# A residual stream kept as fp32 tiles and updated in place, sums over h made from six classical tiles on, and the last output group by token halves

## The chip, the cores and the metric

The kernel runs on one core of one Trainium2 chip. The metric is the device time of one execution in microseconds (us). Before the change three runs gave 1734.82, 1736.02 and 1736.64 us; the median is 1736.02 us. Times in the trace are counted from the first instruction of one profiled execution of the same kernel.

## The reference, cut to what matters

A trunk of two layers over 528 tokens (16 meta tokens and 512 of the input) with 1024 channels, all in float32. Each layer has a mixer and an MLP, and after each of the four sublayers the stream is scaled, added to and normalized:

```python
DN_ALPHA = (2 * DEPTH) ** 0.25

def sq_relu_mlp(h, w1, w2):
    return jnp.square(jax.nn.relu(h @ w1)) @ w2        # w1 1024 x 4096, w2 4096 x 1024

for i in range(DEPTH):
    if i % 2 == 0:
        mix = retention_gdn_mixer(h, ...)              # retention heads and gated DeltaNet heads
    else:
        mix = mamba2_mixer(h, ...)                     # SSD
    h = layer_norm(DN_ALPHA * h + mix, ln1_w[i], ln1_b[i])
    h = layer_norm(DN_ALPHA * h + sq_relu_mlp(h, mlp_w1[i], mlp_w2[i]), ln2_w[i], ln2_b[i])
return h[:, N_META:]
```

## The kernel before, in words

**Numbers.** A value is kept as two rounded fp32 parts, hi and lo (`split`, L152 and L153: ScalarE casts hi, VectorE subtracts it to get lo). A product of two such values is three matmuls, hi by hi, hi by lo and lo by hi (`mm3`, L172 to L174). The activations lie with channels on the 128 partitions and tokens along the row: eight tiles `hh`/`hl` of 528 tokens. Layer 0 works in token halves of 272 and 256 tokens; from `wo1` on in layer 1 it is 256 and 256 (the 16 meta tokens are dropped), and there a matmul can take all 512 columns at once.

**Weights.** SyncE loads a weight tile of 128 x 1024 from HBM into a raw buffer of pool "w" (`fetch`, L160); `halve` then makes a hi and a lo buffer out of it, in the same pool. So a weight tile of 1024 columns takes three of the 12 buffers while it is split, and two until its last matmul. The normalizing rows (`row`) lie in a pool of 3 buffers of their own, and the work tiles `m` in a pool of 24.

**Order.** The code is one program text in which background tasks (generators) advance at each `tick`. A scheduler then lays the instructions of each engine in one fixed order, under the limits of the pools: a tile that finds no free buffer comes later in that order. Each engine works its own list strictly in that order; a row that waits holds up every row behind it on that engine. SyncE's list of DMA issues is such a list too.

**Norm** (`norm_after`). For each token half: transposes of the residual tiles (L270), statistics (L272, L294), scaled rows (L321 and L322), transposes back (L330), then hi by ScalarE (L337), the fp32 value by VectorE (L339) and lo by GpSimd or VectorE (L340). The residual `alpha * h` is rebuilt from hi and lo in `residual` (L354 and L355 ahead of time, or L366 and L367 at the first partial sum; later sums are added by L362).

**MLP** (`mlp`). The hidden layer of 4096 is cut into 8 groups of 4 tiles. Groups 0 and 1 are computed classically: w1 tiles 0 to 3 (the first three of them by token halves, held, as `head=3`), then for each tile of group 1 the tile itself and two output tiles of w2 for group 0 (`second(0, ...)`). From group 2 on, two hidden tiles at a time are computed by a scheme of seven products in place of eight (`Unit`, its matmuls at L500); for it VectorE and GpSimd make four sums over h for each of four row pairs (`combos`, L386 to L401, 16 sums, each split into hi and lo, called `tt`) and four sums over the weights (L473 to L477). A unit's first product needs a weight part and h alone; its second needs the weight sum s2 and the sums over h. Between units stand `Four` stages: four output tiles of w2 for the group before. The last group's output (`second(NG - 1, ..., tail=3)`) takes five tiles whole and the last three by token halves, so that the norm of half 0 runs beside the products of half 1.

**Around it.** The mixer of layer 0 has 40 weight tiles of 1024 x 128 and ends with `wo0` (8 output tiles with two weight loads each, the last two by token halves, `tail=2`); GDN's triangular solve goes through HBM (`da`, `dt`, `du`, L776 to L813, with rows in pool "row"). The SSD mixer of layer 1 reads rows of decay factors back from HBM (`rd`, L1171), and ends with `wo1`.

Of the kernel before, what the change touches and what calls it, by code (L numbers as in the profile page):

```python
# [18 lines left out]
P = 128  # L19
# [38 lines left out]
def trunk(ctx: ExitStack, tc: tile.TileContext, a, out):  # L58
# [11 lines left out]
    NBUF = {"s": 40, "m": 24, "n": 40, "row": 3}  # L70
# [84 lines left out]
    def wtile(dt=F32R):  # L155
        return sb.tile([P, 1024], dt, tag="w", bufs=12, name=nm("w"))
# [152 lines left out]
    def norm_after(r, ns, wcol, bcol):  # L309
# [5 lines left out]
        def task(hf):  # L315
            n, norm = ns[hf], []

            def apply(off, bn, pt, mean, rstd):
                row = tl("row", 1024)
                t2 = [row[:, j * 512:(j + 1) * 512] for j in range(2)]  # L320
                S.activation(t2[1][:bn], pt[1][:bn, :], AF.Identity, bias=shift(mean, rstd, bn), scale=rstd)  # L321
                V.tensor_scalar(t2[0][:bn], pt[0][:bn, :], mean, rstd, op0=SUB, op1=MUL)  # L322
# [4 lines left out]
            for m in range(KT):  # L327
# [10 lines left out]
                t = tl("m", n)  # L338
# [7 lines left out]
    def residual(hx, offs, ns, early=()):  # L346

        r, pre = [{}, {}], [{}, {}]
        for m in early:
            for hf in range(2):  # L350
                n, off = ns[hf], offs[hf]
                hi, lo = hx[hf][m]
                t = tl("m", n)
                V.tensor_scalar(t, hi[:, off:off + n].bitcast(F32), DN_ALPHA, None, op0=MUL)  # L354
                V.scalar_tensor_tensor(t, lo[:, off:off + n].bitcast(F32), DN_ALPHA, t, op0=MUL, op1=ADD)  # L355
                pre[hf][m] = t

        def evac(m, hf, o, last=True):
            n, off = ns[hf], offs[hf]
            if m in pre[hf]:  # L360
                t = pre[hf][m]
                V.tensor_tensor(t, t, o, op=ADD)  # L362
            else:
                hi, lo = hx[hf][m]
                t = pre[hf][m] = tl("m", n)
                V.scalar_tensor_tensor(t, hi[:, off:off + n].bitcast(F32), DN_ALPHA, o, op0=MUL, op1=ADD)  # L366
                V.scalar_tensor_tensor(t, lo[:, off:off + n].bitcast(F32), DN_ALPHA, t, op0=MUL, op1=ADD)  # L367
# [4 lines left out]
    def combos(pairs, nh, get):


        q = slice(0, nh), slice(nh, 2 * nh)

        def part(k, c, lo):
            return pairs[k][lo][:, q[c]].bitcast(F32)

        def diff(out, a, b, engine):  # L380
            engine.tensor_tensor(out, a, b, op=SUB)

        for k in range(4):
            d1, d3, e = tl("m", nh), tl("m", nh), tl("m", nh)
            G.tensor_tensor(d1, part(k, 1, 0), part(k, 0, 0), op=SUB)
            V.tensor_tensor(e, part(k, 1, 1), part(k, 0, 1), op=SUB)  # L386
            V.tensor_tensor(d1, d1, e, op=ADD)
            get(0, k, d1)
            yield
            G.tensor_tensor(d3, part(k + 4, 1, 0), part(k, 1, 0), op=SUB)  # L390
            V.tensor_tensor(e, part(k + 4, 1, 1), part(k, 1, 1), op=SUB)
            V.tensor_tensor(d3, d3, e, op=ADD)
            get(2, k, d3)
            yield
            d2, d4 = tl("m", nh), tl("m", nh)
            G.tensor_tensor(d2, part(k + 4, 1, 0), d1, op=SUB)
            V.tensor_tensor(d2, d2, part(k + 4, 1, 1), op=ADD)
            get(1, k, d2)
            yield
            G.tensor_tensor(d4, part(k + 4, 0, 0), d2, op=SUB)  # L400
            V.tensor_tensor(d4, d4, part(k + 4, 0, 1), op=ADD)  # L401
            get(3, k, d4)
            yield

    def mlp(l, hx, ns, ready, r, evac0, pairs):
# [155 lines left out]
        u, ev = group()  # L561
        phase([([w1[l, f]], f) for f in range(GF)], hx, ev, ns, head=3, ready=ready)
        spawn(combos(pairs, nh, get))
        stages = []
        un, evn = group()
        groups = [(u, ev), (un, evn)] + [group() for _ in range(2, NG)]
# [213 lines left out]
    def gdn_base():  # L780
# [3 lines left out]
        bt, tb, ub = [tl("row", n * n, part=68) for _ in range(3)]  # L784
# [19 lines left out]
        tms = [tl("row", 1024) for _ in range(2)]  # L804
# [317 lines left out]
    r, ev = residual(h, (0, 0), ns0, early=range(5, KT))  # L1122
# [40 lines left out]
    def ssd_group(g, f, ys):  # L1163
# [5 lines left out]
        def loads(c):  # L1169
            rw = tl("row", 1024)  # L1170
# [177 lines left out]
    r, ev = residual(h, (16, 0), ns1, early=range(5, KT))  # L1348
# [18 lines left out]
    r, ev = residual(h, (0, 0), ns1)  # L1367
# [3 lines left out]
    def finish(hf):  # L1371
# [5 lines left out]
        def whole(off, bn, pt, mean, rstd):  # L1377
            row = tl("row", 1024)
# [34 lines left out]
    mlp(1, h, ns1, ready, r, ev, hp)  # L1413
# [101 lines left out]
```

## Time and profile before

| what | value |
|---|---|
| median of the runs shown | 1736.02 us |
| the profiled execution | 1738.46 us |
| its span, first to last instruction | 1736.7 us |
| around the span | 1.8 us |
| mean granted TensorE clock | 0.982 |
| DMA, over the span | 158.05 MB, 91 GB/s |

The profile's page gives first the busy time of each engine: PE is TensorE's matmuls, PEld its weight loads, DVE VectorE, ACT ScalarE, POOL GpSimd, SP SyncE. A row of a timeline has the start, the duration, the engine, the line of the kernel, the operation, the tiles written and read, and how many records were put together; in brackets stands the idle time ahead of it and what ended it. A row of the windows has, for a stretch of time, its length, the busy time of PE, PEld, DVE, ACT and POOL with counts, the granted clock as a share of full speed, the busy share of the DMA engines and GB/s.

### The profile page before, as it was taken

To read this page: it belongs to the slowest core of one execution; us is meant where nothing else is said; L and a number is where in the kernel's file an instruction comes from. 1 tells how busy PE (TensorE), PEld (TensorE's weight loads), DVE (VectorE), ACT (ScalarE), POOL (GpSimd) and SP (SyncE) were. 2 spreads that over 40 slices of the span, in tenths; PEclk is the share of its full clock that TensorE was granted. 3 is DMA by queue.
4 is the path that set the end of the run, shared out by engine and by line. 5 is a ranking of instruction groups with operands and counts; after the bars stand their busy time and mean duration, and the time that the engine had idled before them with its cause. 6 is when DMAs were issued, how large, how long until landed. Compare 5 with 4: busy or idle time off the path is not lost.

```text
span 1736.7 us, 30064 instructions
## 1 busy us (share of the span) xinstructions
PE 1674.2 (96%) x11896; PEld 1542.2 (89%) x11896; DVE 1199.8 (69%) x2383; ACT 700.9 (40%) x1354; POOL 351.1 (20%) x412
## 2 busy tenths in 40 slices
PE   9998999999999899999999998999999998999997
PEld 7897998899999889999998987888778987888886
DVE  5896666766437877767747876767564688777765
ACT  4432235554214344444424643545432434444431
POOL 1211210010003411111102145344410342111112
PEclk9998999999999999999999999999999999999999
DMA  7223212112222232222221443333223123222321
GB/s 243 82 91 86 88 47 84 46 54 84 87 74 68 73 104 98 98 98 98 79 71 62 137 121 92 102 112 98 91 67 110 55 91 110 98 98 98 101 73 69
DMA packets 93002, 158.05 MB, mean 91 GB/s; under 512 B 14077, under 2 KB 47229, under 8 KB 92605
## 3 DMA queue, kind: packets, MB, share of 16 engines
q1 hardware_dynamic: 92716, 155.87, 27.9%
q8 instruction: 93, 1.52, 0.4%
q14 instruction: 49, 0.39, 0.1%
q10 hardware_dynamic: 144, 0.26, 0.0%
HBM read 149.95 MB, written 6.15 MB: 90 GB/s over the span
## 4 chain that ended last, share of the span: by engine, by line
PE 79%; DVE 10%; DMA 4%; POOL 3%; ACT 2%; issue 2%; SPq 0%; POOLq 0%; DVEq 0%; ACTq 0%
PE pmm L172 18%; PE pmm L174 18%; PE pmm L173 18%; PE pmx L500 10%; PE pmm L500 4%; DVE w L153 2%; DVE s L603 2%; DMA row<-rd 1%; DMA w<-in_w 1%; PE pmx L1241 1%; PE pmx L270 1%; DMA du<-row 1%; POOL n L147 1%; PE pmx L1245 1%; ACT w L152 1%
## 5 line engine op out<-in xcount | busy, mean ns | idle before, releaser
L172 PE MATMUL pmm<-hh,w 128*128 128x256 f32 (+5 forms) x1528 | 472.9, 310 | 5.6 <-DVE m L366 2.8
L174 PE MATMUL pmm<-hh,w 128*128 128x256 f32 (+5 forms) x1528 | 459.4, 301 | 2.1 <-DVE w L153 2.1
L173 PE MATMUL pmm<-hl,w 128*128 128x256 f32 (+5 forms) x1528 | 458.4, 300 | 0.7 <-POOL hl L340 0.3
L153 DVE TENSOR_TENSOR w<-w,w 128x1024 fp32r<-128x1024 f32 (+2 forms) x269 | 323.7, 1205 | 142.0 <-PE pmm L173 67.6
L152 ACT CAST w<-w 128x1024 fp32r<-128x1024 f32 (+2 forms) x269 | 263.7, 981 | 373.7 <-PE pmm L174 137.1
L172 PE MATMUL pmm<-s,w 128*128 128x256 f32 (+2 forms) x1180 | 376.8, 319 | 4.3 <-DVE m L366 2.7
L174 PE MATMUL pmm<-s,w 128*128 128x256 f32 (+2 forms) x1180 | 375.5, 318 | 0.2 <-DVE w L153 0.2
L173 PE MATMUL pmm<-s,w 128*128 128x256 f32 (+2 forms) x1180 | 375.5, 318 | 0.0
L172 PEld LDWEIGHTS pmm<-hh,w 128*128 128x128 f32 (+2 forms) x1528 | 289.1, 189 | 20.9 <-issue 4.0
L173 PEld LDWEIGHTS pmm<-hl,w 128*128 128x128 f32 (+2 forms) x1528 | 289.0, 189 | 13.5 <-issue 2.4
L174 PEld LDWEIGHTS pmm<-hh,w 128*128 128x128 f32 (+2 forms) x1528 | 289.0, 189 | 11.4 <-DVE w L153 2.9
L172 PEld LDWEIGHTS pmm<-s,w 128*128 128x128 f32 x1180 | 222.3, 188 | 20.1 <-DVE m L366 3.2
L174 PEld LDWEIGHTS pmm<-s,w 128*128 128x128 f32 x1180 | 222.2, 188 | 15.8 <-DVE w L153 0.6
L173 PEld LDWEIGHTS pmm<-s,w 128*128 128x128 f32 x1180 | 222.2, 188 | 15.2 <-DVE s L1320 0.3
L435 POOL TENSOR_TENSOR m<-m 128x256 f32<-128x256 f32 (+2 forms) x128 | 89.0, 697 | 511.7 <-ACT m L433 499.4
L362 DVE TENSOR_TENSOR m<-m,pmm 128x256 f32<-128x256 f32 (+1 forms) x236 | 93.6, 416 | 71.7 <-PE pmm L174 71.5
L147 POOL TENSOR_TENSOR n<-n,neg 128x1 f32<-128x1 f32 (+2 forms) x58 | 39.8, 690 | 450.4 <-DVE n L146 426.4
L603 DVE SCALAR_TENSOR_TENSOR s<-s,pp,s 128x528 f32<-128x528 f32 x120 | 101.3, 844 | 33.4 <-ACT s L601 31.1
L442 DVE TENSOR_TENSOR s<-m,s 128x256 fp32r<-128x256 f32 (+2 forms) x128 | 69.5, 546 | 51.1 <-POOL m L435 49.9
L500 PE MATMUL pmx<-s,s 128*128 128x264 f32 (+1 forms) x576 | 75.4, 287 | 5.6 <-ACT s L152 5.3
L500 PEld LDWEIGHTS pmx<-s,s 128*128 128x128 f32 x576 | 72.5, 192 | 6.1 <-ACT s L152 5.5
L500 PE MATMUL pmx<-s,w 128*128 128x264 f32 (+1 forms) x576 | 77.6, 284 | 0.0
(312 smaller groups left out, 2368.1 us busy)
## 6 DMA issues: line engine op xcount, KB each, us to landing
w<-in_w SPq DMA_DIRECT2D x88, 512.0 KB, 3.3
w<-in_mw SPq DMA_DIRECT2D x176, 256.0 KB, 3.0
w<-in_mw SPq DMA_DIRECT2D x40, 512.0 KB, 3.2
w<-in_wo SPq DMA_DIRECT2D x29, 512.0 KB, 3.4
row<-rd SPq DMA_DIRECT2D x16, 512.0 KB, 5.7
s<-rd SPq DMA_DIRECT2D x32, 128.0 KB, 5.5
out<-row SPq DMA_DIRECT2D x7, 256.0 KB, 2.0
w<-in_wo SPq DMA_DIRECT2D x6, 256.0 KB, 2.5
```

Source lines behind the costliest of these rows:

```text
L147: G.tensor_tensor(dst, t, neg5[0:part, 0:n], op=POW)
L152: S.copy(dst_hi, src)
L153: V.tensor_tensor(dst_lo, src, dst_hi.bitcast(F32), op=SUB)
L172: T.matmul(o, w[0], x[0], start=first, stop=False)
L173: T.matmul(o, w[0], x[1], start=False, stop=False)
L174: T.matmul(o, w[1], x[0], start=False, stop=last)
L270: T.transpose(pt[m // 4][:bn, (m % 4) * P:(m % 4 + 1) * P], r[m][:, off:off + bn], ident)
L362: V.tensor_tensor(t, t, o, op=ADD)
L435: G.tensor_tensor(q, t, t, op=MUL)
L442: V.tensor_tensor(lo, q, hi.bitcast(F32), op=SUB)
L500: T.matmul(o, w[x][:, c], B[b][k][y], start=first and k == i == 0, stop=last and k == 3 and i == 2, skip_group_check=True)
L603: V.scalar_tensor_tensor(acc, cin[:, k:k + L], w[k], acc, op0=MUL, op1=ADD)
```

## The change

Eight fp32 tiles `R` of 128 x 528 hold the residual stream from start to end. They are loaded with the input, the first partial sum of a sublayer does `R = alpha * R + sum` in one VectorE instruction, later ones add, and the norm writes its fp32 result back into them. The sums over h are then made from R by four VectorE instructions for each row pair, none on GpSimd. For the room, pool "m" goes from 24 to 19 buffers, and pool "row" (3) is merged with pool "w" (12) into one of 13. In the MLP only six w1 tiles stay classical (group 0, and tiles 0 and 2 of group 1); tiles 1 and 3 of group 1 become a 13th unit, and the output of group 0 moves behind it into two `Four` stages. The last group's weights are prepared as `Four` stages are, and all eight of its output tiles go by token halves.

```diff
-    NBUF = {"s": 40, "m": 24, "n": 40, "row": 3}
+    NBUF = {"s": 40, "m": 19, "n": 40, "w": 13}
...
-        return sb.tile([P, 1024], dt, tag="w", bufs=12, name=nm("w"))
+        return sb.tile([P, 1024], dt, tag="w", bufs=NBUF["w"], name=nm("w"))
...
+    R = [sb.tile([P, L], F32, tag="r", bufs=KT, name=nm("r")) for _ in range(KT)]
...
-            raw = tl("m", n)
+            raw = R[k][:, o:o + n]
...
-                row = tl("row", 1024)
+                row = tl("w", 1024)
...
-                t = tl("m", n)
+                t = r[hf][m]
                 V.tensor_scalar(t, pf, w, b, op0=MUL, op1=ADD)
...
         def evac(m, hf, o, last=True):
-            n, off = ns[hf], offs[hf]
-            if m in pre[hf]:
-                t = pre[hf][m]
+            t = R[m][:, offs[hf]:offs[hf] + ns[hf]]
+            if (m, hf) in seen:
                 V.tensor_tensor(t, t, o, op=ADD)
             else:
-                hi, lo = hx[hf][m]
-                t = pre[hf][m] = tl("m", n)
-                V.scalar_tensor_tensor(t, hi[:, off:off + n].bitcast(F32), DN_ALPHA, o, op0=MUL, op1=ADD)
-                V.scalar_tensor_tensor(t, lo[:, off:off + n].bitcast(F32), DN_ALPHA, t, op0=MUL, op1=ADD)
+                V.scalar_tensor_tensor(t, t, DN_ALPHA, o, op0=MUL, op1=ADD)
+                seen.add((m, hf))
...
+    def combos(off, nh, get):
 
         for k in range(4):
...
+            q0, q1 = [[R[i][:, off + c * nh:off + (c + 1) * nh] for c in range(2)] for i in (k, k + 4)]
+            d = [tl("m", nh) for _ in range(4)]
+            V.tensor_tensor(d[0], q0[1], q0[0], op=SUB)
+            V.tensor_tensor(d[2], q1[1], q0[1], op=SUB)
+            V.tensor_tensor(d[1], q1[1], d[0], op=SUB)
+            V.tensor_tensor(d[3], q1[0], d[1], op=SUB)
...
+        stages = [unit(1, 1), four(0, 0), four(0, 1)]
         for c in range(2, NG):
...
-        for f in range(GF):
-            phase([([w1[l, GF + f]], f)], hx, evn, ns)
-            if f == 2:
-                spawn(stages[0].gen)
-            second(0, u, 2 * f, 2 * f + 2)
+            stages += [unit(c, 0), four(c - 1, 0), unit(c, 1), four(c - 1, 1)]
+        last = [four(NG - 1, 0), four(NG - 1, 1)]
+        gens = [st.gen for st in stages + last]
+        phase([([w1[l, f]], f) for f in range(GF)], hx, groups[0][1], ns, head=3, ready=ready)
+        spawn(combos(off, nh, get))
+        phase([([w1[l, GF]], 0)], hx, groups[1][1], ns)
+        spawn(gens[0])
+        phase([([w1[l, GF + 2]], 2)], hx, groups[1][1], ns)
         until(lambda: "s4" in stages[0].ops and all(x is not None for y in tt for x in y))
...
-        second(NG - 1, groups[-1][0], 0, KT, tail=3)
+        blks = last[0].blks + last[1].blks
+        phase([([[blks[m]]], m) for m in range(KT)], groups[-1][0], evac0, ns, tail=KT)
...
-        zero = tl("row", 731)
+        zero = tl("w", 731)
...
-        bt, tb, ub = [tl("row", n * n, part=68) for _ in range(3)]
+        bt, tb, ub = [tl("w", n * n, part=68) for _ in range(3)]
...
-            rw = tl("row", 1024)
+            rw = tl("w", 1024)
```

The same rename from "row" to "w" is made in the output's norm. Over the whole program TensorE streams 3,223,300 matmul columns in place of 3,229,540; VectorE has 2281 instructions in place of 2365, ScalarE 1293 in place of 1301, GpSimd 385 in place of 417.

**TensorE at the end of wo0, where the MLP of layer 0 begins.** In this list `pmm_6352` of before (`pmm_6306` of the change) is the last output tile of wo0, `pmx` with `cst` are transposes of the norm for token half 1, and `hh`/`hl` with `w` are the MLP's w1 products. Before, in the order of TensorE:

```order
L270 MATMUL pmx_6473<-cst,m_5391 128x128
L172 MATMUL pmm_6352<-s_5353,w_6194 128x256
L173 MATMUL pmm_6352<-s_5354,w_6194 128x256
L174 MATMUL pmm_6352<-s_5353,w_6195 128x256
L172 MATMUL pmm_6538<-hh_6381,w_6534 128x272
L173 MATMUL pmm_6538<-hl_6382,w_6534 128x272
L174 MATMUL pmm_6538<-hh_6381,w_6535 128x272
```

The change, the same place:

```order
L174 MATMUL pmm_6306<-s_5345,w_6149 128x256
L272 MATMUL pmx_6408<-cst,r_81 128x128
...
L332 MATMUL pmx_6517<-cst,w_6468 128x128
L332 MATMUL pmx_6523<-cst,w_6468 128x128
...
L332 MATMUL pmx_6559<-cst,w_6468 128x128
L332 MATMUL pmx_6559<-cst,w_6473 128x128
L172 MATMUL pmm_6484<-hh_6335,w_6480 128x272
```

Before, three w1 half tiles (72 matmuls, `pmm_6538`, `pmm_6638`, `pmm_6677`) stand between wo0's last matmul and the end of the norm's transposes of half 1; in the change none does, and `pmm_6484` follows the last transpose. Its weight's hi part, on ScalarE, and lo part, on VectorE, stand among the norm's rows of half 1 (ScalarE: behind the sixth of eight hi rows).

**VectorE in the classical phase of the MLP, layer 0, the change.** `L414` makes the lo part of a hidden tile's square and so waits for that tile's products; `s_6847` is made from `pmm_6817`, the first half of the fifth of six classical w1 tiles and the ninth of their twelve half tiles on TensorE. `L441` to `L445` are the unit's weight sums, `L368` to `L371` the sums over h.

```order
L153 TENSOR_TENSOR w_7055<-w_6956,w_7054 128x1024
L414 TENSOR_TENSOR s_6847<-m_6844,s_6846 128x272
L368 TENSOR_TENSOR m_6850<-r_75 128x264
L369 TENSOR_TENSOR m_6852<-r_79,r_75 128x264
L370 TENSOR_TENSOR m_6851<-r_79,m_6850 128x264
...
L371 TENSOR_TENSOR m_7029<-r_82,m_7027 128x264
L153 TENSOR_TENSOR s_7037<-m_7027,s_7037 128x264
L153 TENSOR_TENSOR w_7106<-w_7062,w_7105 128x1024
L153 TENSOR_TENSOR s_7041<-w_6957,s_7040 128x512
```

All 16 sums over h stand behind that `L414`; from the first of them to `s_7041`, the lo part of the weight sum s2, there are 36 rows: 16 sums, 14 of their splits, 3 rows `L414`, one row `L445`, the split of `w_7106` and that of s2 itself, which is the last. In layer 1 the list has the same form with 256 columns; there the second `L414` row of `s_16052`, which waits for the last of the six classical tiles, stands in the middle of it, and 17 rows follow it up to the lo part of s2 (7 sums, 7 of their splits, one `L445`, the split of a 1024-column weight and that of s2). Before, the sums of a layer are spread over the list between the rows of eight w1 and eight w2 tiles.

**SyncE in layer 0's mixer.** `da` is the scratch of GDN's solve in HBM, and `w` from `in_w` are weight tiles. The change:

```order
L749 DMA da<-s_938 128x4x128
L758 DMA w_981<-da 68x32x32
L160 DMA w_1053<-in_w 128x1024
L160 DMA w_1150<-in_w 128x1024
L160 DMA w_1249<-in_w 128x1024
```

Before, the load of the same weight tile, there `w_1061`, stands ahead of the writes:

```order
L160 DMA w_1061<-in_w 128x1024
L160 DMA w_1158<-in_w 128x1024
L776 DMA da<-s_734 128x4x128
...
L776 DMA da<-s_946 128x4x128
L160 DMA w_1495<-in_w 128x1024
L785 DMA row_989<-da 68x32x32
```

Six weight loads that stood ahead of the read of `da` stand behind it. They are `w_1061`, `w_1158`, `w_1257`, `w_1352`, `w_1420` and `w_1495` before, `w_1053` to `w_1487` in the change.

More of the change, by code (lines that the diff above doesn't have):

```diff
@@ L370, in residual, with mlp @@
         return r, evac
[L372 to L381, printed above, removed]
-        for k in range(4):
[L384 to L405, printed above, removed]
+    def combos(off, nh, get):
+        for k in range(4):
+            q0, q1 = [[R[i][:, off + c * nh:off + (c + 1) * nh] for c in range(2)] for i in (k, k + 4)]
[4 more added lines that the diff above has]
+            V.tensor_tensor(d[3], q1[0], d[1], op=SUB)
+            for j in range(4):
+                get(j, k, d[j])
+                if j % 2:
+                    yield
+    def mlp(l, hx, off, ns, ready, evac0, pairs):
         w1, w2 = a["mw1"], a["mw2"]
@@ L559, in run, with unit, four @@
                             adv()
[L561 to L566, printed above, removed]
-        for c in range(2, NG):
-            for i in range(2):
-                stages.append(Unit(c, i, lambda f, hf, o, e=groups[c][1]: e(f, hf, o, nh)))
-                stages.append(Four(c - 1, groups[c - 1][0], 4 * i))
-        for f in range(GF):
-            phase([([w1[l, GF + f]], f)], hx, evn, ns)
-            if f == 2:
-                spawn(stages[0].gen)
-            second(0, u, 2 * f, 2 * f + 2)
+        groups = [group() for _ in range(NG)]
+        def unit(c, i):
+            return Unit(c, i, lambda f, hf, o: groups[c][1](f, hf, o, nh))
+        def four(c, i):
+            return Four(c, groups[c][0], 4 * i)
+        stages = [unit(1, 1), four(0, 0), four(0, 1)]
+        for c in range(2, NG):
+            stages += [unit(c, 0), four(c - 1, 0), unit(c, 1), four(c - 1, 1)]
[6 more added lines that the diff above has]
+        phase([([w1[l, GF + 2]], 2)], hx, groups[1][1], ns)
         until(lambda: "s4" in stages[0].ops and all(x is not None for y in tt for x in y))
@@ L803, in gdn_base @@
         yield from pause(2)
-        tms = [tl("row", 1024) for _ in range(2)]
+        tms = [tl("w", 1024) for _ in range(2)]
         for hd in range(4):
@@ L1121, in trunk @@
     ns0 = (272, 256)
-    r, ev = residual(h, (0, 0), ns0, early=range(5, KT))
+    r, ev = residual((0, 272), ns0)
     hn, hp, ready = norm_after(r, ns0, PP_LN, PP_LN + 8)
@@ L1125, in trunk @@
     h = hn
-    r, ev = residual(h, (0, 0), ns0)
+    r, ev = residual((0, 272), ns0)
     hn, hx, ready1 = norm_after(r, ns0, PP_LN + 16, PP_LN + 24)
-    mlp(0, h, ns0, ready, r, ev, hp)
+    mlp(0, h, 0, ns0, ready, ev, hp)
     h = hn
@@ L1347, in trunk @@
     srcs = [[a["wo1"][m, :, 0:1024], a["wo1"][m, :, 1024:2048]] for m in range(KT)]
-    r, ev = residual(h, (16, 0), ns1, early=range(5, KT))
+    r, ev = residual((16, 272), ns1)
     hn, hp, ready = norm_after(r, ns1, PP_LN + 32, PP_LN + 40)
@@ L1366, in trunk @@
     h = hn
-    r, ev = residual(h, (0, 0), ns1)
+    r, ev = residual((16, 272), ns1)
     normed = [False, False]
@@ L1377, in whole @@
         def whole(off, bn, pt, mean, rstd):
-            row = tl("row", 1024)
+            row = tl("w", 1024)
             t0, t1 = row[:, 0:512], row[:, 512:1024]
@@ L1388, in last @@
         def last(blocks):
-            t = [[x[:, 0:512], x[:, 512:1024]] for x in (tl("row", 1024), tl("row", 1024))]
+            t = [[x[:, 0:512], x[:, 512:1024]] for x in (tl("w", 1024), tl("w", 1024))]
             (o0, p0, m0, n0, s0), (o1, p1, m1, n1, s1) = blocks
@@ L1412, in trunk @@
     spawn(finish(1))
-    mlp(1, h, ns1, ready, r, ev, hp)
+    mlp(1, h, 16, ns1, ready, ev, hp)
     drain()
```

30 lines of the change are left out of this document (10 added, 20 removed).

## The prediction

> **What bounds the kernel now.** The page comes first: its busy times and its chain of work.
>
> ```profile
> span 1736.7 us, 30064 instructions
> PE 1674.2 (96%) x11896; PEld 1542.2 (89%) x11896; DVE 1199.8 (69%) x2383; ACT 700.9 (40%) x1354; POOL 351.1 (20%) x412
> PE 79%; DVE 10%; DMA 4%; POOL 3%; ACT 2%; issue 2%; SPq 0%; POOLq 0%; DVEq 0%; ACTq 0%
> ```
>
> TensorE is busy for 1674.2 of 1736.7 us, so about 62 us of the span are gaps. A change gains only by fewer matmul columns or fewer gaps. Next, the view that lists TensorE's waits by what it waited for: the largest single ones.
>
> ```profile
> PE pmx L1006 <- ACT m L1027: 8.0, 1, 8.0
> PE pmm L172 <- DVE m L366: 5.6, 5, 1.5
> PE pmx L500 <- ACT s L152: 5.3, 1, 5.3
> ```
>
> The first lies in layer 0's mixer, the second in the classical part of layer 0's MLP, the third at the first unit of layer 1's MLP. The windows show what stands beside them.
>
> ```profile
> 150.00:160.00 10.00, 2.42 (x18) 2.09 (x16) 0.79 (x3) 1.10 (x2) 0.00 (x0) 0.74 0.74 214
> ...
> 590.00:600.00 10.00, 8.55 (x68) 8.13 (x67) 10.00 (x23) 3.84 (x9) 4.36 (x6) 1.00 0.01 2
> 600.00:610.00 10.00, 6.57 (x48) 5.75 (x46) 9.58 (x17) 3.20 (x7) 4.66 (x6) 1.00 0.22 79
> 610.00:620.00 10.00, 6.58 (x32) 6.37 (x33) 5.95 (x12) 2.56 (x5) 0.17 (x1) 0.66 0.08 26
> ...
> 1430.00:1440.00 10.00, 7.43 (x37) 5.80 (x35) 8.92 (x18) 3.66 (x8) 5.05 (x6) 1.00 0.58 190
> 1440.00:1450.00 10.00, 6.80 (x36) 6.50 (x37) 8.95 (x19) 4.63 (x8) 0.73 (x1) 0.66 0.07 25
> ```
>
> In the classical part of both MLPs VectorE is the limit (10.00 and 9.58 of 10 us at 590 to 610, with TensorE down to 6.57). The column of the granted clock shows a second price: after a gap of some microseconds the clock stands at 0.66 over 10 us, so 3.4 us are not granted, part of them inside the gap. I charge 2.6 us of half clock for a long gap (bounds 1.7 and 3.4).
>
> **Matmuls.** The chain gives a unit's products; two starts of a 512-column tile give the classical step.
>
> ```profile
> 693.69 1.46 PE pmm L500 x12
> 695.15 4.41 PE pmx L500 x36
> ...
> 1507.77 1.41 PE pmm L500 x12
> 1509.18 4.26 PE pmx L500 x36
> ...
> 1430.02 0.39 PE L172 MATMUL pmm<-s,w 128*128 128x512 f32 x1
> 1430.25 0.40 PE L173 MATMUL pmm<-s,w 128*128 128x512 f32 x1
> ```
>
> One matmul of a unit takes 4.41/36 = 0.122 us in layer 0 and 4.26/36 = 0.118 us in layer 1; 512 columns take about 0.225 us (0.23 between these starts, 0.22 and 0.23 alternating). The 13th unit is 84 matmuls. It replaces 96 of about 0.122 in layer 0 (11.7 to 10.2, gain 1.5) and 48 of 0.225 in layer 1 (10.8 to 9.9, gain 0.9). The last group of layer 1 by halves takes 24 x 0.118 = 2.83 in place of 12 x 0.225 = 2.70 us a tile; five more tiles do so: **+0.7**. These gains are inside the two sums below.
>
> **From the norm into the MLP, layer 0.** The order shows that no w1 product stands any more beside the norm of half 1: 72 matmuls, some 9 us, that covered it have moved behind its last transpose, because raw, hi and lo of the first weight find no free buffer among 13 while wo0's last two tiles hold eight and the norm's rows the others. What the norm takes is in the trace:
>
> ```profile
> 539.95 0.29 PE L172 MATMUL pmm<-hh,w 128*128 128x272 f32 x1
> ...
> 541.11 0.40 DVE L362 TENSOR_TENSOR m<-m,pmm 128x256 f32<-128x256 f32 x1
> 541.43 1.21 DVE L153 TENSOR_TENSOR w<-w,w 128x1024 fp32r<-128x1024 f32 x1
> ...
> 544.38 1.03 ACT L152 CAST w<-w 128x1024 fp32r<-128x1024 f32 x1
> 548.89 3.76 ACT L337 ACTIVATE hh<-pmx,pp 128x256 fp32r<-128x256 f32 x8 [0.33 <-PE pmx L330]
> ```
>
> Before, TensorE went from wo0 to w1 at 539.95. From the last evacuation at 541.11 to the first hi row is 7.8 us. The change takes the weight split of 1.21 us out of that stretch, and transposes no longer queue behind products (0.7, an estimate): first hi row at 547.0. Six hi rows (6 x 0.47 = 2.8), the weight's cast (1.03) and its split (1.21 less overlap) put the first full w1 step at **551.7**. That is a gap of almost 10 us with only transposes in it; I charge 2.0 us of clock. Twelve half tiles of 24 matmuls at 0.1225 (between 256 and 272 columns), 12 x 2.94 = 35.3 us, then end at 589.0, and the unit's first product (1.5) at 590.5.
>
> **The unit's second product, layer 0.** It needs the sums over h and s2. VectorE reaches them only behind the `L414` of the ninth half tile: 551.7 + 2.0 + 9 x 2.94 = 580.2, plus 1.4 us for relu, square and lo. Then come 36 rows. Their price:
>
> ```profile
> 582.39 0.42 DVE L386 TENSOR_TENSOR m<-hl 128x264 f32<-128x264 f32 x1
> 582.73 0.43 DVE L367 SCALAR_TENSOR_TENSOR m<-hl,m 128x272 f32<-128x272 f32 x1
> 583.09 0.42 DVE L387 TENSOR_TENSOR m<-m,m 128x264 f32<-128x264 f32 x1
> ...
> 585.13 0.68 DVE L153 TENSOR_TENSOR w<-w,w 128x512 fp32r<-128x512 f32 x1
> 585.73 0.87 DVE L153 TENSOR_TENSOR s<-m,s 128x264 fp32r<-128x264 f32 x1
> ...
> L153 DVE TENSOR_TENSOR s<-m,s 128x264 fp32r<-128x264 f32 x11 | 5.4, 502 | 0.5 <-ACT s L152 0.5
> ```
>
> A row of 264 columns takes 0.42 us and the next begins 0.35 after it; a 512-column split 0.60, a 1024-column one 1.13 by the same measure. 33 rows x 0.345 + 2 x 0.60 + 1.13 = 13.7 us. In the same phase the splits average 0.502 us beside GpSimd (one row above: 0.87), so I add 1.8: 15.5 us (bounds 13.7 and 36 x 0.502 = 18). s2 is ready at 597.1. TensorE waits from 590.5: **6.6 us**, 2.6 of clock, then 72 matmuls (8.8) and eight w2 tiles of 24 (23.3, four of them already done in the gap, 0.5 less). Group 2 begins at 631.3. Before:
>
> ```profile
> 627.57 0.28 PE L500 MATMUL pmm<-hh,w 128*128 128x264 f32 x1
> ...
> 1367.23 0.40 DVE L362 TENSOR_TENSOR m<-m,pmm 128x256 f32<-128x256 f32 x1
> 1373.42 3.76 ACT L337 ACTIVATE hh<-pmx,pp 128x256 fp32r<-128x256 f32 x8 [0.27 <-PE pmx L330]
> ...
> 1437.36 0.28 PE L500 MATMUL pmm<-hh,w 128*128 128x256 f32 x1
> 1442.93 0.79 PE L500 MATMUL pmx<-s,s 128*128 128x256 f32 x2 [5.30 <-ACT s L152]
> ```
>
> Layer 0: 631.3 - 627.6 = **+3.7 us** (range -2 to +9). This already counts that the old gaps of 590 to 614 are gone.
>
> Three or four of GpSimd's squares fall into that stretch. The Trainium skill, SBUF — State Buffer, section "SBUF: two separate sides", says that VectorE with two SBUF inputs and GpSimd lock a shared port for a whole instruction. The 0.87 us row above agrees with it. By it, GpSimd's 32 subtractions that leave would free VectorE, the 1.8 us would go in each layer, and the sum would be 3.6 us lower; it would still be positive.
>
> **The same in layer 1.** Hi rows began at 1373.42; with the split out, 1372.3, plus 2.8, 1.03 and 0.8: first step at 1376.9. Six half tiles (24 x 0.118) and three of 512 columns (24 x 0.225) are 33.2 us; with 2.0 of clock they end at 1412.1, the first product at 1413.5. Here the list puts 17 rows of sums behind the `L414` of the **last** classical tile, so they cannot begin before 1412.1 + 1.5: 14 x 0.345 + 2 x 0.60 + 1.13 = 7.2, with GpSimd 8.5, ready at 1422.1. Wait 8.6, clock 2.6, 8.5 for 72 matmuls, 21.6 for w2, less 0.9 done in the gap: group 2 begins at 1453.9. Before, its first unit's first product ended with the matmul at 1437.36 and so began 11 x 0.118 earlier, at 1436.06; behind it 5.3 us and about 2.5 of half clock were lost: 1443.9. Difference **+10.0 us** (range +4 to +14).
>
> **The mixer of layer 0.** Six weight loads now queue on SyncE behind the read of `da`, which waits for the last write.
>
> ```profile
> 81.39 0.37 PE L172 MATMUL pmm<-hh,w 128*128 128x272 f32 x1
> ...
> 84.50 0.37 SPq L776 DMA_DIRECT2D da<-s  x1
> 86.89 0.32 SPq L785 DMA_DIRECT2D row<-da  x1
> 138.50 5.03 SPq L802 DMA_DIRECT2D du<-row  x1
> ...
> w<-in_w SPq DMA_DIRECT2D x88, 512.0 KB, 3.3
> ```
>
> VectorE has about 6 us less ahead of that write (the residual's and weight rows that move), so 78.5, 2.4 more to the read, 3.3 to land, 2 to split: 86, where before that tile's products began at 81.4, with some 3 us of other products moved ahead of it. That is 2 to 8 us lost, and half clock. Against it, the 8.0 us gap at 152 to 160 (the `du` write waits for VectorE) and its 2.4 of clock shrink or go, since TensorE comes later and VectorE earlier. Sum **-2** (range -8 to +5).
>
> **The rest.** The first SSD weights queue behind reads of `rd` that share the pool now: **+1.5** (0 to +5). The last group's norm of half 0 lies beside eight half tiles in place of three: **-1** (-2 to 0). Between MLP 0 and SSD the cover of half 0 grows and that of half 1 goes; I charge 0 (-3 to +3). Steady units keep 12 or 13 buffers: 0, since the weights are asked for several stages ahead there. The new adds in place cost VectorE one instruction where two stood, and lie behind matmuls: 0.
>
> **Sum.** 3.7 + 10.0 + 0.7 - 2 + 1.5 - 1 = +12.9 us on the profiled execution of 1738.46: 1751.4. The median of the runs is 2.4 lower, so I predict **1749 us**.
>
> **The rivals.**
> - *The sums come in time* (faster). If VectorE's 36 rows end before 590.5 and 17 before 1413.5, both waits with their clock go: -6.6 - 2.6 - 8.6 - 2.6 = -20.4, hence 1749 - 20.4 = 1729. It decides where VectorE begins the sums 7 us earlier than the order's rows let me think. For it: VectorE has 84 instructions fewer. Against it: `L414` stands ahead, and in layer 1 even the last tile. 13%.
> - *SyncE's queue becomes the bound* (slower than forecast). Loads behind `da` and `rd` stop TensorE in the mixer and in SSD at the upper bounds, +5 and +5 in place of -2 and +1.5, and the 36 rows take 18 us (+2.5 in each layer): 1749 + 15.5 = 1764. 15%.
> - *The change moves cover and no time*: the old gaps give back 8.0 + 2.4 at 152, 8.3 (the idle part of the three windows from 590) + 2.6, and 5.3 + 2.5, together 29 us; the two new waits of sums (20.4) and what the norm's uncovered chain costs beyond its half clock eat just that if a norm wait is 4 us in place of almost 10, which needs the first weight to find its buffers 6 us earlier than the order has it. Then 1749 - 2 x 6 = 1737. 10%.
> - The forecast: 62%, by itself 1741 to 1758.
>
> The range 1732 to 1763 holds the forecast, the third rival and parts of the first two. A difference under 0.2% is about what a measurement of this kernel can tell from none. From the cases: faster 0.14, same 0.10, slower 0.76.
>
> **What would show it.** In the profile after: a gap of TensorE of 7 to 10 us before the first w1 product in both MLPs, ended by ScalarE or VectorE's weight part; a wait of `L500`'s second product of 6 to 9 us in both, ended by VectorE; the granted clock below 1 behind each; no gap at 590 to 614 and a smaller one at 152. A VectorE that reaches the sums by 574 would make it wrong, or a first w1 step before 547.

## The result, and the profile after

The changed kernel takes 1751.3 us, median of 4 runs (1749.31 to 1753.46), where the kernel before took 1735.91 in the same rounds. The ratio is 1.0089, 95% interval 1.0072 to 1.0107: slower by 15 us. The profiled execution took 1749.31 us, with a span of 1747.4, 10.7 us more than the span before. The page of the changed kernel begins:

```profile
span 1747.4 us, 30083 instructions
PE 1675.7 (96%) x11980; PEld 1543.4 (88%) x11980; DVE 1173.6 (67%) x2299; ACT 692.7 (40%) x1346; POOL 333.6 (19%) x380
PE 76%; DVE 10%; issue 6%; POOL 3%; ACT 3%; DMA 2%; SPq 0%; POOLq 0%; DVEq 0%; ACTq 0%
```

VectorE's busy time fell by 26 us and GpSimd's by 17.5, and the kernel is slower all the same: less work on these engines does not by itself shorten TensorE's path. TensorE's waits by what it waited for, the same kernel (in a row: the total in us, how many waits, the longest):

```profile
PE pmm L172 <- ACT w L152: 9.2, 5, 4.0
PE pmx L332 <- DVE n L308: 8.0, 3, 2.7
PE pmx L468 <- ACT s L152: 5.6, 2, 3.0
PE pmx L839 <- DVE e L836: 3.6, 1, 3.6
```

The long waits of before (8.0 us in the mixer, the 5.6 of `L366`) are gone. In their place stand waits for a weight's hi part (`L152`), for the norm's chain (`L308`, three times, once for each of three norms) and for the unit's split sums. TensorE's timeline at the first MLP shows them in order; the columns are start, duration, engine, line, operation, tiles, and in brackets the idle time ahead and what ended it.

```profile
541.01 0.76 PE L272 MATMUL pmx<-cst,r 128*128 128x128 f32 x3 [0.16 <-DVE n L274]
544.49 0.41 PE L332 MATMUL pmx<-cst,w 128*128 128x128 f32 x2 [2.72 <-DVE n L308]
...
550.40 0.39 PE L172 MATMUL pmm<-hh,w 128*128 128x272 f32 x1 [1.11 <-ACT w L152]
551.90 0.39 PE L174 MATMUL pmm<-hh,w 128*128 128x272 f32 x1 [0.98 <-DVE w L153]
...
588.50 0.29 PE L468 MATMUL pmm<-hh,w 128*128 128x264 f32 x1
...
590.86 0.39 PE L468 MATMUL pmm<-hh,w 128*128 128x264 f32 x1 [0.74 <-ACT w L472]
...
596.07 0.51 PE L468 MATMUL pmx<-s,s 128*128 128x264 f32 x2 [3.00 <-ACT s L152]
597.27 0.60 PE L174 MATMUL pmm<-s,w 128*128 128x272 f32 x1 [0.69 <-DVE w L153]
...
628.80 0.28 PE L468 MATMUL pmm<-hh,w 128*128 128x264 f32 x1
```

From 540.6, where wo0 ends, to 550.4 there are only transposes. The windows of this kernel beside it (length, busy PE, PEld, DVE, ACT, POOL, clock, DMA share, GB/s), first MLP and second:

```profile
540.00:550.00 10.00, 5.57 (x27) 3.51 (x25) 7.17 (x20) 4.98 (x9) 3.29 (x6) 0.83 0.15 54
550.00:560.00 10.00, 8.62 (x54) 8.40 (x55) 6.17 (x9) 4.44 (x9) 3.79 (x5) 0.83 0.17 54
...
590.00:600.00 10.00, 5.57 (x32) 5.04 (x31) 9.50 (x22) 6.60 (x14) 0.56 (x1) 0.84 0.24 79
...
1370.00:1380.00 10.00, 5.13 (x21) 3.06 (x20) 7.30 (x21) 5.36 (x10) 3.71 (x6) 0.66 0.13 39
...
1420.00:1430.00 10.00, 6.61 (x32) 5.59 (x33) 10.00 (x23) 6.48 (x14) 0.00 (x0) 0.83 0.31 98
```

Before, the gap lay at 590 to 620 with VectorE full; now there are two in each MLP, one in the chain of the norm, with VectorE busy for 7.17 and 7.30 of 10 us, and one with VectorE full again. A third gap of the norm's kind lies between the MLP of layer 0 and SSD; it is shown below.

For all runs the span is cut at the same places of the program: in wo0's norm, where the transposes of half 0 go on after its last residual tile is done (521.2 us before; its first twelve transposes came earlier, at 478.6), at the first matmul of the first unit of group 2 in layer 0, at the first transposes of wo1's norm, and at the end. So stage A is the mixer of layer 0 up to wo0's norm, B that norm and the MLP's start, C the rest of layer 0 and SSD, D the second norm, its MLP and the end. Times are of one profiled execution each; kernels whose lists are alike in a stage differ there by up to 2 us (A of the change, e1 and e4; C of the change and e1).

| kernel | A | B | C | D | span | ratio of the times to before, interval |
|---|---|---|---|---|---|---|
| before | 521.2 | 106.4 | 708.2 | 400.9 | 1736.7 | |
| the change | 522.3 | 106.5 | 710.4 | 408.2 | 1747.4 | 1.0089 (1.0072 to 1.0107) |
| e1: unit later | 522.6 | 103.3 | 711.9 | 403.4 | 1741.2 | 1.0024 (1.0015 to 1.0034) |
| e4: last three by halves | 520.5 | 107.6 | 720.5 | 409.9 | 1758.5 | 1.0136 (1.0121 to 1.0151) |
| e2: rows in a pool of their own | 521.1 | 99.1 | 702.6 | 398.4 | 1721.2 | 0.9925 (0.9911 to 0.9938) |
| e5: only the norm's rows so | 530.4 | 96.9 | 714.5 | 397.5 | 1739.3 | 1.0019 (1.0009 to 1.0028) |
| e6: rows behind two weight tiles | 522.8 | 100.6 | 707.4 | 404.1 | 1734.9 | 1.0001 (0.9990 to 1.0012) |
| e3: e1 and e2 | 522.6 | 95.3 | 702.5 | 391.9 | 1712.3 | 0.9862 (0.9847 to 0.9878) |
| e8: e3, one buffer more | 523.5 | 97.5 | 708.9 | 391.4 | 1721.3 | 0.9914 (0.9901 to 0.9928) |
| e7: e2 with twelve units | 522.4 | 95.6 | 699.5 | 398.5 | 1716.0 | 0.9900 (0.9887 to 0.9914) |
| e9: e7, last three by halves | 523.5 | 96.1 | 705.5 | 400.2 | 1725.3 | 0.9932 (0.9919 to 0.9946) |

Differences between run times below are taken between these ratios; a thousandth is 1.74 us. By their intervals such a difference is uncertain by 3 to 4 us. The stages are of single executions and need not add up to it: from before to the change they give 10.7 us, where the ratio gives 15.

### The profile page after: what moved, and what is told of

Read it like the earlier page. It is cut to its first block, busy times and chain, and to the rows that moved or that the text cites. A ratio compares the mean times of both kernels' runs of the same rounds, so it can differ in the third digit from the quotient of the medians.

```text
span 1747.4 us, 30083 instructions
## 1 busy us (share of the span) xinstructions
PE 1675.7 (96%) x11980; PEld 1543.4 (88%) x11980; DVE 1173.6 (67%) x2299; ACT 692.7 (40%) x1346; POOL 333.6 (19%) x380
## 4 chain that ended last, share of the span: by engine, by line
PE 76%; DVE 10%; issue 6%; POOL 3%; ACT 3%; DMA 2%; SPq 0%; POOLq 0%; DVEq 0%; ACTq 0%
PE pmm L174 17%; PE pmm L172 17%; PE pmm L173 17%; PE pmx L468 10%; PE pmm L468 4%; DVE s L576 2%; DVE w L153 2%; DMA w<-in_w 1%; PE pmx L272 1%; POOL w L1154 1%; ACT w L152 1%; POOL n L147 1%; PE pmx L332 1%; DVE r L341 1%; DVE n L274 1%
## 5 line engine op out<-in xcount | busy, mean ns | idle before, releaser
L172 PE MATMUL pmm<-hh,w 128*128 128x256 f32 (+3 forms) x1480 | 457.2, 309 | 10.5 <-ACT w L152 9.2
L174 PE MATMUL pmm<-hh,w 128*128 128x256 f32 (+3 forms) x1480 | 443.3, 300 | 4.4 <-DVE w L153 4.4
L173 PE MATMUL pmm<-hl,w 128*128 128x256 f32 (+3 forms) x1480 | 442.8, 299 | 0.1
L152 ACT CAST w<-w 128x1024 fp32r<-128x1024 f32 (+2 forms) x253 | 257.6, 1030 | 179.5 <-DMA w<-in_wo 77.8
L172 PEld LDWEIGHTS pmm<-hh,w 128*128 128x128 f32 (+1 forms) x1480 | 280.0, 189 | 25.9 <-ACT w L152 10.4
L174 PEld LDWEIGHTS pmm<-hh,w 128*128 128x128 f32 (+1 forms) x1480 | 279.5, 189 | 14.2 <-DVE w L153 5.6
L173 PEld LDWEIGHTS pmm<-hl,w 128*128 128x128 f32 (+1 forms) x1480 | 280.2, 189 | 10.9 <-issue 2.7
L174 PEld LDWEIGHTS pmm<-s,w 128*128 128x128 f32 x1200 | 226.0, 188 | 16.4 <-DVE w L153 1.8
L172 PEld LDWEIGHTS pmm<-s,w 128*128 128x128 f32 x1200 | 226.1, 188 | 15.5 <-ACT s L1292 0.9
L173 PEld LDWEIGHTS pmm<-s,w 128*128 128x128 f32 x1200 | 226.0, 188 | 15.1 <-DVE s L1293 0.8
L407 POOL TENSOR_TENSOR m<-m 128x256 f32<-128x256 f32 (+2 forms) x128 | 93.8, 733 | 556.5 <-ACT m L405 551.7
L576 DVE SCALAR_TENSOR_TENSOR s<-s,pp,s 128x528 f32<-128x528 f32 x120 | 115.0, 958 | 16.6 <-ACT s L574 14.7
L355 DVE TENSOR_TENSOR r<-r,pmm 128x256 f32<-128x256 f32 (+1 forms) x224 | 89.4, 417 | 47.3 <-PE pmm L174 46.9
L414 DVE TENSOR_TENSOR s<-m,s 128x256 fp32r<-128x256 f32 (+2 forms) x128 | 64.1, 502 | 62.7 <-POOL m L407 56.0
L472 ACT COPY w<-pmm 128x264 f32<-128x264 f32 (+1 forms) x26 | 9.8, 375 | 234.8 <-PE pmm L468 234.8
L468 PE MATMUL pmm<-hh,w 128*128 128x264 f32 (+1 forms) x416 | 83.5, 283 | 2.7 <-ACT w L472 2.7
```

Of the source, the lines that this page charges most:

```text
L152: S.copy(dst_hi, src)
L172: T.matmul(o, w[0], x[0], start=first, stop=False)
L173: T.matmul(o, w[0], x[1], start=False, stop=False)
L174: T.matmul(o, w[1], x[0], start=False, stop=last)
L407: G.tensor_tensor(q, t, t, op=MUL)
L414: V.tensor_tensor(lo, q, hi.bitcast(F32), op=SUB)
```

## The experiments

The theory was that the loss has two causes in each MLP: the norm of half 1 lost its cover, and the 13th unit waits for its sums. Rivals: the waits only move on, or the cover is lost for want of buffers.

**e1: the unit later.** One stage of output tiles goes ahead of the 13th unit; the wait for the sums moves with it.

```diff
-        stages = [unit(1, 1), four(0, 0), four(0, 1)]
+        stages = [four(0, 0), unit(1, 1), four(0, 1)]
...
+        until(lambda: len(stages[0].blks) == 4)
...
+            if i == 1:
+                until(lambda: all(x is not None for y in tt for x in y))
```

> The changed kernel with one edit: the first of the two output stages of group 0 stands ahead of the 13th unit, so that 96 matmuls (11.7 us in layer 0, 10.8 in layer 1) lie between the last classical w1 tile and the unit that needs the sums over h. Theory A (the unit stands too early for sums that VectorE can only make behind the last classical tiles): TensorE's waits at the unit's second product (about 6.5 us in layer 0 and 7 in layer 1, and 1.6 us of half clock each) go, so 13 to 17 us less than the changed kernel: 1734 to 1738. Rival B (VectorE has too much work in the classical phase wherever the unit stands, so the wait moves to the evacuations of the output stage or to the next unit): 1747 to 1751.

Measured 1742.36 us, ratio 1.0024: 6.5 thousandths, 11.3 us, under the change's ratio. B is 3.2 us shorter and D 4.8. The wait at the unit of layer 0 is gone; a smaller one is at the evacuations of the stage ahead of it, in VectorE's list behind the sums. Its timeline of TensorE:

```profile
595.51 0.38 PE L172 MATMUL pmm<-s,w 128*128 128x256 f32 x1 [1.59 <-DVE r L357]
599.54 0.39 PE L172 MATMUL pmm<-s,w 128*128 128x256 f32 x1 [0.86 <-DVE r L357]
```

By the ratios the gain is a little below theory A's 13 to 17 us; the time itself lies between the two ranges, and the two profiled executions differ by 6.2 us only. Most of the wait goes, and these 2.5 us of it have moved, as B had it. e3 against e2 repeats the edit and gives 10.9 us.

**e2: rows in a pool of their own**, with 13 buffers in all as before.

```diff
-    NBUF = {"s": 40, "m": 19, "n": 40, "w": 13}
+    NBUF = {"s": 40, "m": 19, "n": 40, "w": 10, "row": 3}
...
-                row = tl("w", 1024)
+                row = tl("row", 1024)
```

All other rows are renamed in the same way.

> The changed kernel with the rows in a pool of their own again (3 buffers), and the weights' pool at 10, so 13 buffers in all as in the change. Theory A (a pool gives out its buffers in program order, so a weight load waits in the list until the norm's rows, whose first writer comes late, have got theirs): the first w1 products of both MLPs come back beside the norm of half 1, and TensorE's gap of 9 to 10 us there and its half clock of about 1.6 us go, twice: 16 to 22 us less than the changed kernel, 1729 to 1735, or up to 5 us more where ten weight buffers are too few elsewhere. Rival B (13 buffers are too few for the weights and the rows together, as the prediction had it): no gain, since no buffer is added; with fewer for weights 1751 to 1760.

Measured 1724.24 us, ratio 0.9925: 28.5 us less than the change, faster than before. With **fewer** buffers for weights the w1 products stand beside the norm again, and TensorE has no gap of more than 0.6 us there. Its windows at the first MLP:

```profile
540.00:550.00 10.00, 9.66 (x79) 9.35 (x78) 7.61 (x20) 4.87 (x9) 2.05 (x4) 1.00 0.17 55
550.00:560.00 10.00, 9.17 (x75) 8.76 (x75) 7.69 (x14) 6.60 (x15) 7.38 (x10) 1.00 0.21 61
```

TensorE is busy 9.66 and 9.17 of 10 us where the change has 5.57 and 8.62, at a clock of 1.00. B is 7.4 and D 9.8 us shorter. The rival, that 13 buffers are too few, is out; a shared pool of more than 13 was not run. The gain is above theory A's range because C is 7.8 us shorter too, which it had left out.

**e5: only the norm's rows** in the pool of 3, all other rows among ten weight buffers. The pools are e2's, and of e2's renames only the one in `norm_after` is made.

> The changed kernel with only the norm's rows in a pool of their own (3 buffers) and all other rows left among the weights (10). Theory A (the norm's rows alone hold up the weight loads behind them): it has nearly all of what a pool for all rows gave, a ratio to the kernel before of 0.991 to 0.995. Rival B (the rows of SSD and of GDN, read back from HBM, are what holds up the loads in the mixers): less than half of it, 1.000 to 1.008.

Measured 1740.27 us, ratio 1.0019. The time is in rival B's range, but by stages each theory has a part. B (96.9) and D (397.5) have all of e2's gain, so in the MLPs the norm's rows alone did it, as theory A had it. C has none of it and A lost 8.1 us. There the rows of GDN and SSD share ten buffers with the weights, fewer than the change's 13, so this run does not tell whether their order or their number costs the time.

**e6: the same pool of 13, another order.** The norm of half 1 pauses between statistics and rows, so that two weight tiles are asked for first.

```diff
             if pend:
+                if hf:
+                    yield from pause(2)
                 apply(*pend.pop())
```

> The changed kernel with its one pool of 13 buffers; the norm's task for half 1 pauses for two steps between its statistics and its rows, so that two weight tiles are asked for ahead of the rows in program order. No buffer is added or set aside. Theory A (order of allocation): 48 of the 72 matmuls come back beside the norm, TensorE's gap ahead of the first w1 step shrinks by 5 to 6 us and its half clock goes in both MLPs: ratio 0.996 to 1.002 against 1.009 of the change. Rival B (too few buffers): no gain, 1.007 to 1.011, or a later norm and a loss.

Measured 1737.38 us, ratio 1.0001, 15.3 us less than the change: theory A. No buffer was added. At the first MLP, TensorE's timeline of this kernel:

```profile
542.98 0.39 PE L174 MATMUL pmm<-hh,w 128*128 128x272 f32 x1 [0.70 <-DVE w L153]
546.54 0.39 PE L174 MATMUL pmm<-hh,w 128*128 128x272 f32 x1 [0.27 <-DVE w L153]
549.41 1.25 PE L334 MATMUL pmx<-cst,w 128*128 128x128 f32 x10
551.10 0.44 PE L334 MATMUL pmx<-cst,w 128*128 128x128 f32 x2 [0.43 <-DVE r L343]
```

Two w1 half tiles, 48 matmuls, run from 541 to 549.4, ahead of the norm's transposes back, which begin at 549.41. The norm itself comes later than in the change (544.49), which is one reason why e6 gains less than e2; the others are not shown (C is 4.8 us longer than e2's, D 5.7, B 1.5).

**e3: both.**

> Both edits: the 13th unit behind one output stage of group 0, and rows in a pool of their own (10 and 3 buffers). Theory A (two separate waits, each with its own cause): the gains add up, 29 to 39 us less than the changed kernel: 1712 to 1722, faster than the kernel before by 0.8 to 1.4%. Rival B (with TensorE earlier by 10 us VectorE becomes the bound of the classical phase as before the change, and one of the gains is given back): 1728 to 1738.

Measured 1714.04 us, ratio 0.9862: 39 us less than the change, and faster than the kernel before by 1.4%. The two edits alone gave 11.3 and 28.5 us, together 39.8: they add up within what a difference can tell, so the two causes are separate. In its page TensorE is busy for 1663.3 of 1712.3 us, 49 us of gaps in place of the change's 72:

```profile
span 1712.3 us, 30155 instructions
PE 1663.3 (97%) x11980; PEld 1537.9 (90%) x11980; DVE 1155.1 (67%) x2299; ACT 697.8 (41%) x1346; POOL 330.5 (19%) x380
```

This is the best version of the study.

**e8: one buffer more.** e3 with 11 weight buffers, and 38 small tiles in place of 40 to make the room.

> Both edits (unit behind one output stage, rows in their own pool) with eleven weight buffers in place of ten, the room taken from the small-tile pool (38 in place of 40). Theory A (order, not room, is what was lost): within 3 us of the run with ten, ratio 0.985 to 0.988. Rival B (room is short): 0.980 to 0.984.

Measured 1722.49 us, ratio 0.9914, 9 us more than e3: neither theory. The stages B and D are within 2.2 us of e3's; C is 6.4 us longer, where SSD uses the small tiles. So an eleventh buffer brought nothing to the MLPs; whether it is worth something in SSD cannot be told from a run that also takes two small tiles away.

**e4: the last group's halves undone.**

```diff
-        phase([([[blks[m]]], m) for m in range(KT)], groups[-1][0], evac0, ns, tail=KT)
+        phase([([[blks[m]]], m) for m in range(KT)], groups[-1][0], evac0, ns, tail=3)
```

> The changed kernel with only the last three output tiles of an MLP's last group by token halves, as before the change. Theory A (by halves costs 0.7 us of columns in layer 1 and hides the norm of half 0 in both layers): slower than the changed kernel by 1 to 4 us, 1752 to 1755. Rival B (the halves cost their columns and hide nothing that was not hidden): 0.7 us faster, 1750 to 1751.

Measured 1761.01 us, ratio 1.0136: 8.2 us more than the change, twice theory A's upper bound. D is 1.7 us longer. C, with the norm between the MLP of layer 0 and SSD, is 10.1 us longer: the halves pay behind the first MLP rather than at the end. Part of it is the norm: the first of SSD's products with a weight tile 128 wide comes 309.4 us into C in the change (938.20) and 313.6 us here (941.65). Where the other 6 us come from, later in SSD, no run tells.

**e7: twelve units, with own rows.** The MLP's old order on top of e2, with R and the halves kept.

> All rows in a pool of their own (10 and 3 buffers), as in the run of that name, but twelve units as before the change: eight classical w1 tiles with the output of group 0 between them; R, the sums from R, and the last group by halves stay. Theory A (in the change as made the 13th unit costs more by its wait for the sums, some 6 us in each MLP, than its columns save, 1.5 and 0.9 us): 4 to 12 us less than with own rows and 13 units, ratio 0.986 to 0.990. Rival B (eight classical tiles keep VectorE the limit there as in the kernel before): no faster, 0.992 to 0.996.

Measured 1719.72 us, ratio 0.9900: 2.5 thousandths, 4.3 us, better than 13 units in the place that the change gave them (e2), and 6.6 us worse than 13 units behind a stage (e3). Theory A, at the low end of its gain, which is hardly more than the uncertainty. By stages e3 is the shorter one in the second MLP alone (D 391.9 against 398.5; B is alike, and C is 3.0 longer). There TensorE waits 5.7 us for lo parts of weights in this run, and not in e3:

```profile
PE pmm L174 <- DVE w L153: 5.7, 3, 2.2
```

So the 13th unit is worth having, but not where it stood, and by these numbers more for this wait than for its fewer columns (0.9 us in layer 1 by the prediction's price).

**e9: R alone.** e7 with the last three tiles by halves, so that of the whole change only the residual stream, the sums made from it and smaller pools are left.

> The residual stream in R and the sums made from it, alone: twelve units and the MLP's order as before the change, the last group with three output tiles by halves as before, rows in a pool of their own (10 and 3 buffers where the kernel before had 12 and 3). Theory A (the halves hide the norm of half 0 behind both MLPs and are worth some 8 us, as the run with the last three tiles by halves showed; R gives the rest of what twelve units with own rows gained): ratio 0.993 to 0.997. Rival B (R's fewer VectorE instructions give nearly all, the halves little without the shared pool): 0.989 to 0.992. Rival C (R alone gives nothing, since the work it saves lay beside matmuls): 0.998 to 1.003.

Measured 1725.55 us, ratio 0.9932: with the smaller pools, R and the sums made from it are worth 11.8 us (theory A), and e7 against e9 gives the halves 5.6 us without the shared pool. Of the stages B alone is much shorter, by 10.3 us. There the old gap is, where VectorE was the limit; windows of e9 at the same place:

```profile
590.00:600.00 10.00, 10.00 (x84) 10.00 (x83) 4.48 (x9) 2.10 (x5) 0.86 (x2) 1.00 0.41 133
600.00:610.00 10.00, 7.87 (x60) 7.23 (x59) 7.97 (x13) 4.23 (x6) 0.39 (x1) 1.00 0.24 79
610.00:620.00 10.00, 10.00 (x84) 10.00 (x84) 5.30 (x11) 3.70 (x8) 1.42 (x2) 1.00 0.42 138
```

TensorE is busy for 27.9 of these 30 us, before for 21.7, and the half clock is gone.

## Why the prediction was right, and where it was not

The median came 2.3 us above the forecast of 1749, by the likeliest case: the two waits that it named are there, in both MLPs. Its reason for the first is wrong, and terms that were mis-sized cancel, so part of the agreement is luck. On the profiled executions the sum was +12.9 and the difference is +10.7. The terms, against the stages:

- **Norm into the MLP, layer 0.** First full w1 step forecast at 551.7, measured at 551.90, in a kernel that reaches this stage 1.1 us later; the gap and its releasers, ScalarE's and VectorE's weight parts, are as told. The **cause** given for it was wrong. The step that failed is "raw, hi and lo of the first weight find no free buffer among 13". The raw tile had one: SyncE issued the first two w1 loads at 526.15 and 529.10 (before: 525.20 and 528.05). What came late is the split, and not the load as e2's theory had it. ScalarE's list, first before, then in the change:

```profile
528.97 1.05 ACT L152 CAST w<-w 128x1024 fp32r<-128x1024 f32 x1 [2.62 <-DMA w<-in_mw]
```

```profile
544.58 1.57 ACT L323 ACTIVATE w<-pmx,n,n 128x512 f32<-128x512 f32 x2 [6.57 <-DVE n L308]
546.57 2.84 ACT L339 ACTIVATE hh<-pmx,pp 128x256 fp32r<-128x256 f32 x6 [0.42 <-PE pmx L332]
549.28 1.07 ACT L152 CAST w<-w 128x1024 fp32r<-128x1024 f32 x1
```

  In the change ScalarE stands idle for 6.57 us, waiting for the norm's statistics, and only behind the norm's rows does it make the weight's hi part, which before it made at 528.97. From 541 on, when wo0's weights have been read, until 549 only six of the 13 buffers hold anything, four raw tiles and two rows, so room does not hold the split there; whether the pool was full earlier, while wo0's last weights lay in it, the trace does not show. In the program's text the norm's rows of half 1 are asked for ahead of the weight's parts, from the same pool (`w_6468` and `w_6473` ahead of `w_6480`), and they are written late, behind the statistics; e2 (ten weight buffers, rows apart) and e6 (the same 13, rows asked for later) have the cover back. How the scheduler comes from that order to these lists was not looked into. The time was right because the order showed the outcome whatever its reason.
- **The unit's wait, layer 0.** s2 was forecast at 597.1 and was ready at 597.82; the product that needs it began at 596.07, with s2's hi part, and went on in full at 598.57. VectorE's list from the first of the sums to s2's lo part:

```profile
582.43 0.43 DVE L368 TENSOR_TENSOR m<-r 128x264 f32<-128x264 f32 x1
...
587.24 0.44 DVE L414 TENSOR_TENSOR s<-m,s 128x272 fp32r<-128x272 f32 x1 [0.53 <-POOL m L407]
...
597.14 0.68 DVE L153 TENSOR_TENSOR s<-w,s 128x512 fp32r<-128x512 f32 x1
```

  These 36 rows took 15.4 us for 15.5 forecast. The 1.8 that the forecast added for GpSimd came about in another way: two waits for GpSimd's squares (0.53 and 0.50 idle) cost most of it, and only one row beside GpSimd was clearly slower (0.73 in place of 0.43). TensorE's wait was mis-sized: 6.6 us were forecast from 590.5, and the brackets hold 0.74, 3.00 and 0.69; the longest is ended by ScalarE, where VectorE was named. Between them stand another product that needs h alone (the 12 matmuls from 590.86, about 1.5 us), which the working left out, and nine matmuls of w2, of which it had four. The charge for half clock was also too high: the twelve half tiles from 551.9 to 588.5 took 36.6 us against 35.3, so about 1.3 in place of 2.0. B came out at +0.1 for a forecast of +3.7: 1.6 us were won up to the unit, counted from where the stage begins, and 2.0 from there to group 2.
- **Layer 1.** Forecast +10.0 for norm and unit, +0.7 for the columns of the halves and -1 for the end, +9.7 together; D is +7.3. e1 and e2 show both parts (4.8 and 9.8 us). The unit's wait is again split, 1.93, 2.59 and 0.68 us, where one of 8.6 was forecast.
- **The mixer of layer 0.** Forecast -2, measured +1.1, within the range and hardly more than the stages differ by. Both effects are there: the gap of 8.0 us at 152 is gone, and new waits between 83 and 96 took its place. The timeline of the changed kernel:

```profile
83.47 1.16 PE L845 MATMUL pmx<-s,s 128*128 128x128 f32 x8 [0.35 <-DVE s L846]
86.61 0.27 PE L833 MATMUL pmx<-cst,s 128*16 128x128 f32 x1 [1.98 <-DVE rq L850]
90.62 1.12 PE L839 MATMUL pmx<-cst,s 128*128 128x128 f32 x4 [3.59 <-DVE e L836]
95.48 0.59 PE L174 MATMUL pmm<-hh,w 128*128 128x272 f32 x1 [1.06 <-DVE w L153]
```

  In e2 six weight loads stand ahead of the read of `da` again (15 in place of 9, as before). None of these waits is there, the old gap is back, and A is 521.1:

```profile
159.61 2.07 PE L979 MATMUL pmx<-s,s 128*128 128x128 f32 x8 [8.18 <-DVE m L1024]
```

- **MLP 0 to SSD.** Forecast 0 and +1.5, measured +2.2 in C, but by terms that were mis-sized and cancel. The forecast charged nothing for this norm, and it is the third that loses its cover: from 924.2 to 932.2 TensorE has only transposes. Windows there, first of the change, then of e2 (8.6 us earlier in its span when C begins):

```profile
920.00:930.00 10.00, 6.66 (x47) 5.43 (x46) 7.05 (x22) 1.53 (x3) 1.70 (x3) 0.90 0.29 104
930.00:940.00 10.00, 8.10 (x45) 6.00 (x44) 7.25 (x13) 6.37 (x12) 4.76 (x10) 0.76 0.16 53
```

```profile
910.00:920.00 10.00, 10.00 (x87) 9.64 (x85) 8.35 (x23) 2.76 (x5) 2.58 (x5) 1.00 0.16 54
920.00:930.00 10.00, 10.00 (x84) 9.54 (x83) 8.43 (x14) 7.16 (x16) 4.85 (x11) 1.00 0.15 55
```

  The change has 5.2 us of idle time and a clock of 0.90 and 0.76, e2 no idle time and a clock of 1.00; its C is 7.8 us shorter. Against that stand the halves, without which C is 10 us longer (e4). The reads of `rd` on SyncE are seen as told, as a small part. First TensorE's row in the timeline of the changed kernel, then SyncE's rows at that place:

```profile
990.00 0.60 PE L172 MATMUL pmm<-hh,w 128*128 128x272 f32 x1 [4.03 <-ACT w L152]
```

```profile
979.76 0.38 SPq L1144 DMA_DIRECT2D w<-rd  x1
980.24 0.53 SPq L160 DMA_DIRECT2D w<-in_w  x1
980.82 0.42 SPq L1144 DMA_DIRECT2D w<-rd  x1
981.34 2.54 SPq L1148 DMA_DIRECT2D s<-rd  x2
983.96 1.10 SPq L160 DMA_DIRECT2D w<-in_w  x1
```

Each weight load stands behind reads of `rd` on SyncE, and TensorE stands 4.03 us for a weight.

- **The rivals.** "The sums come in time" is what e1 builds on purpose. It gave 11.3 us where the rival's price was 20.4, for the two reasons named (a filled wait and a smaller charge for the clock). "SyncE's queue becomes the bound" is there in the waits between 83 and 96 and at 990, and did not set the time: A is +1.1 and C +2.2. "The change moves cover and no time" needed a norm wait of 4 us; from 540.6 to 550.4 it is almost 10. GpSimd's share of the sums' time was not tried by itself; the one slower row above speaks for a small one in the change.

The change holds three gains (R 11.8 us, halves 5.6 to 8.2, the 13th unit 6.6 where it does not wait) and two losses that outweigh them: one pool for rows and weights, 28.5 us, and the unit's place, 10.9 (e2 against e3) to 11.3. The steps from before over e9, e7, e3 and e2 to the change are these five, so 11.8 + 5.6 + 6.6 - 10.9 - 28.5 gives the measured 15 by construction. What checks them is e1 and e4, which make a step in another place and find 11.3 for 10.9 and 8.2 for 5.6.

## What to carry to other kernels

Tiles that are asked for early in the program but written late do not belong in one pool with tiles that are to be loaded ahead: the later ones queue behind them. Here it was the order that cost, not the number of buffers. Work that needs sums made beside a phase goes one independent stage behind that phase. A sum of terms that comes out right is no proof of its terms, so the stages are compared one by one, and the kernel that looks like a failure may be two edits from the best one.

## What the runs showed of the hardware

The price of half clock after the same gap was not the same in two executions. e1 has the change's gap ahead of the first w1 step, with the norm's rows alike, and its window 550 to 560 shows a granted clock of 0.65 where the change shows 0.83:

```profile
550.00:560.00 10.00, 8.73 (x47) 8.41 (x48) 5.99 (x9) 4.18 (x7) 3.96 (x5) 0.65 0.17 54
```

That is 1.8 us of clock, enough to blur single profiles of stage B.
